# Weights by pairs of column blocks, TensorE in program order, and half of the low parts by ScalarE and an accumulating DMA

## The chip, the cores and the metric

One core of one Trainium2 chip. The metric is the device time of the program in microseconds; the time before is 2558.9 us, the median of three runs (2558.71 to 2560.08).

## The reference

One layer of a decoder trunk on 256 tokens of width 2048 (batch 1), in float32:

```python
h = x + 0.5 * swiglu(rmsnorm(x, ffn1_norm), ffn1_w_gu, ffn1_w_down)      # width 5632
proj = rmsnorm(h, mix_norm) @ w_in                                     # u | v | z | x B C | dt
a_out = chunked_sgu(gelu(u), gelu(v), gm_v_norm, gm_w_s, gm_b_s)        # causal, chunks of 128
m_out = mamba2_group(z, xbc, dt, ...)                                  # conv, scan of 32 heads, gate, norm
h = h + concat([a_out, m_out]) @ w_out
h = h + memory_cross_attention(rmsnorm(h), rmsnorm(mem), w_q, w_kv, w_o)  # 4 heads, 256 memory tokens
h = h + 0.5 * swiglu(rmsnorm(h, ffn2_norm), ffn2_w_gu, ffn2_w_down)
return rmsnorm(h, final_norm)
```

Nearly all the work is `activations @ weights` with 256 rows of activations; some 460 MB of weights are read once from HBM.

## The kernel before, in words

**Arithmetic.** A matrix product in float32 is made of three products in the faster type float32r. Each operand is split exactly into a high part (rounded to float32r) and a low part (the rest): x·w = xh·wh + xh·wl + xl·wh. Weights are split on the fly in `split` (L110): ScalarE copies the raw tile to the high part `whi` (L119), VectorE subtracts it from the raw tile and gives the low part `wlo` (L120). Activations are split when they are transposed to an operand (`to_operand`, L186).

**Tiles.** `load` (L100) brings four k-tiles of 128 rows by 512 columns, 1 MB, into one of three `raw` buffers with one DMA on SyncE's queue. `split` makes two `whi` and two `wlo` tiles of it, each [128, 2, 512]: two k-tiles of one column block. There are four buffers of `whi` and four of `wlo`, so two megabytes are split at a time.

**Projections.** `proj_tok` (L131) computes one block of 512 columns for both token tiles (128 tokens each): for each group of four k-tiles, for each k-tile and token tile, the matmuls of L147 (xh, wh), L148 (xh, wl) and L149 (xl, wh) into the token tile's PSUM bank; the stationary operand is a 128x128 tile of x, the weights move. `proj_feat` (L153) puts features on partitions: the weights are the stationary operand and the 256 tokens move (L164 to L168).

**Order.** The feed-forward parts (`ffn`, L236) alternate a gate block (SiLU by ScalarE, L246) and an up block (product by VectorE, L250), transpose the product to the operand `hid` (L192), and after six or five such blocks project down onto the four 512-column chunks of the residual stream `h`. The mixers use 16 blocks of `w_in` token-wise or feature-wise, with the scan, the gating weights and small transposes between; then `w_out`, the cross attention, and the second feed-forward part with the final norm (`finish`, L667). The program names tiles and dependences; the framework's scheduler orders each engine's instructions by a model of their times and adds the semaphores. TensorE's order is therefore the scheduler's: transposes and small products may be moved among the projections' matmuls. GpSimd makes constants, the powers for the norms (L182), and issues a few loads (`dec` L433, `wn` L518, `mem` L576, `fw` L669).

Of the kernel before, what the change touches and what calls it, by code (L numbers as in the profile page):

```python
# [16 lines left out]
P = 128  # L17
D = 2048
S = 256
# [14 lines left out]
KG = 4  # L34
LOG1P_TERMS = 9

# columns of the packed per-partition parameters
# [8 lines left out]
def hybrid_layer(ctx: ExitStack, tc: tile.TileContext, x, mem, w_gu1, w_dn1, w_in, w_s, w_out,  # L46
# [12 lines left out]

    def slot(shape, dtype, name):  # L60
        return big.tile(shape, dtype, name=name, tag="slot")
# [38 lines left out]
    def load(w, r0, n0, pieces=1):  # L100
        raw = wraw.tile([P, KG, NC], F32, name="raw")
        src = w[r0:r0 + KG * P, n0:n0 + NC].rearrange("(k p) n -> p k n", p=P)
        st = KG // pieces
        for j in range(0, KG, st):
            nc.sync.dma_start(out=raw[:, j:j + st, :], in_=src[:, j:j + st, :])
        return raw

    last_hi = [None]

    def split(raw, behind=None):  # L110
        # behind: for each half, instructions of ScalarE and VectorE to queue it behind
        parts = []
        for j in range(0, KG, 2):
            hi = wsp.tile([P, 2, NC], F32R, name="whi")
            lo = wsp.tile([P, 2, NC], F32R, name="wlo")
            with ExitStack() as order:
                for ins in behind[j // 2] if behind else ():
                    order.enter_context(tc.issue_after(ins))
                last_hi[0] = nc.scalar.copy(out=hi, in_=raw[:, j:j + 2, :]).ins  # L119
                nc.vector.tensor_tensor(out=lo, in0=raw[:, j:j + 2, :], in1=hi.bitcast(F32), op=ALU.subtract)  # L120
            parts.append((hi, lo))
        return parts
# [3 lines left out]
    def load_split(w, r0, n0):  # L126
        key = (id(w), r0, n0)
        return split(*ready.pop(key)) if key in ready else split(load(w, r0, n0))

    # Operands in xts: tiles [P, KG, 2 * S] with the high parts of S tokens, then the low parts.  # L130
    def proj_tok(w, r0, xts, n0, apart=0):  # L131
        # the last `apart` groups run token tile by token tile
        ps = [mm.tile([P, NC], F32, name="acc") for _ in range(NT)]
        groups = [[g] for g in range(len(xts) - apart)]
        if apart:
            groups.append(list(range(len(xts) - apart, len(xts))))
        for gs in groups:
            parts = {g: load_split(w, r0 + g * KG * P, n0) for g in gs}
            order = [(t, g, k) for g in gs for k in range(KG) for t in range(NT)]
            if len(gs) > 1:  # L140
                order.sort()
            for t, g, k in order:
                hi, lo = parts[g][k // 2]
                first, last = g == 0 and k == 0, g == len(xts) - 1 and k == KG - 1
                xh = xts[g][:, k, t * P:(t + 1) * P]
                xl = xts[g][:, k, S + t * P:S + (t + 1) * P]
                nc.tensor.matmul(ps[t], lhsT=xh, rhs=hi[:, k % 2, :], start=first, stop=False)  # L147
                nc.tensor.matmul(ps[t], lhsT=xh, rhs=lo[:, k % 2, :], start=False, stop=False)  # L148
                nc.tensor.matmul(ps[t], lhsT=xl, rhs=hi[:, k % 2, :], start=False, stop=last)  # L149
        return ps  # L150

    # Features on partitions: two tiles of [P, 2, S], for four groups of 128 features.
    def proj_feat(w, xts, n0):  # L153
        ps = [mm.tile([P, 2, S], F32, name="acc") for _ in range(2)]
        for g, xt in enumerate(xts):
            parts = load_split(w, g * KG * P, n0)
            for k in range(KG):
                hi, lo = parts[k // 2]
                first, last = g == 0 and k == 0, g == len(xts) - 1 and k == KG - 1
                for c in range(4):  # L160
                    cs = slice(c * P, (c + 1) * P)
                    o = ps[c // 2][:, c % 2, :]
                    # one accumulation group for both halves of a bank
                    nc.tensor.matmul(o, lhsT=hi[:, k % 2, cs], rhs=xt[:, k, :S], start=first and c % 2 == 0,  # L164
                                     stop=False)
                    nc.tensor.matmul(o, lhsT=hi[:, k % 2, cs], rhs=xt[:, k, S:], start=False, stop=False)  # L166
                    nc.tensor.matmul(o, lhsT=lo[:, k % 2, cs], rhs=xt[:, k, :S], start=False,  # L167
                                     stop=last and c % 2 == 1)  # L168
        return ps

# [14 lines left out]
    # 512 columns of NT token tiles -> one split operand tile, scaled per feature  # L185
    def to_operand(srcs, dst, c0=None):  # L186
        done = []
        for q in range(0, KG, 2):
            ps = side("tpose").rearrange("p (k s) -> p k s", k=2)
            for k in range(2):  # L190
                for t in range(NT):
                    nc.tensor.transpose(out=ps[:, k, t * P:(t + 1) * P],  # L192
                                        in_=srcs[t][:, (q + k) * P:(q + k + 1) * P], identity=ident)
            if c0 is None:
                hi = nc.scalar.copy(out=dst[:, q:q + 2, :S], in_=ps)
                lo = nc.vector.tensor_tensor(out=dst[:, q:q + 2, S:], in0=ps,
                                             in1=dst[:, q:q + 2, :S].bitcast(F32), op=ALU.subtract)
            else:
                for k in range(2):
                    sc = col[:, c0 + q + k:c0 + q + k + 1]  # L200
                    hi = nc.scalar.activation(dst[:, q + k, :S], ps[:, k, :], AF.Copy, scale=sc)
                    lo = nc.vector.scalar_tensor_tensor(out=dst[:, q + k, S:], in0=ps[:, k, :], scalar=sc,
                                                        in1=dst[:, q + k, :S].bitcast(F32),
                                                        op0=ALU.mult, op1=ALU.subtract)
            done.append((hi.ins, lo.ins))
        return done

    class Normed:
        """The next norm's operand, made chunk by chunk as the residual stream gets ready."""
# [5 lines left out]
        def chunk(self, n):  # L215
            self.operand(n)
            self.stats(n)

        def operand(self, n):
            dst = slot([P, KG, 2 * S], F32R, f"xt_{self.name}{n}")  # L220
            self.xts.append(dst)
            return to_operand([h[n][:, t, :] for t in range(NT)], dst, self.c0 + n * KG)
# [7 lines left out]
    def residual(n, ps, scale):  # L230
        for t in range(NT):
            nc.vector.scalar_tensor_tensor(out=h[n][:, t, :], in0=ps[t], scalar=scale, in1=h[n][:, t, :],
                                           op0=ALU.mult, op1=ALU.add)

# [1 line left out]
    def ffn(nrm, w_gu, w_dn, done, before=None, closing=False):  # L236
        for c_from, c_to in ((0, 6), (6, 11)):
            hts = []
            for c in range(c_from, c_to):
                pg = proj_tok(w_gu, 0, nrm.xts, c * NC)  # L240
                if c == 0 and before is not None:
                    before()
                gs = []
                for t in range(NT):
                    g = half_k(F32, "gate")
                    nc.scalar.activation(g, pg[t], AF.Silu, scale=nrm.rstd[:, t:t + 1])  # L246
                    gs.append(g)
                pu = proj_tok(w_gu, 0, nrm.xts, DFF + c * NC)
                for t in range(NT):
                    nc.vector.scalar_tensor_tensor(out=gs[t], in0=pu[t], scalar=nrm.rstd[:, t:t + 1],  # L250
                                                   in1=gs[t], op0=ALU.mult, op1=ALU.mult)
                dst = slot([P, KG, 2 * S], F32R, "hid")
                to_operand(gs, dst)
                hts.append(dst)
            for n in range(4):
                pd = proj_tok(w_dn, c_from * NC, hts, n * NC, apart=2 if closing and c_to == 11 and n == 3 else 0)
                residual(n, pd, 0.5)
                if c_to == 11:
                    done(n)

    n1 = Normed("ffn1", C_FFN1)
    for n in range(4):
        for t in range(NT):
            nc.sync.dma_start(out=h[n][:, t, :], in_=x_v[:, t, n * NC:(n + 1) * NC])
        if n < 3:
# [452 lines left out]
```

## Time and profile before

| | |
|---|---|
| median of three runs | 2558.9 us |
| span of the profiled execution | 2557.8 us |
| TensorE busy, matmuls | 2539.3 us (99%), 12990 |
| VectorE busy | 1375.6 us (54%) |
| ScalarE busy | 1164.2 us (46%) |
| GpSimd busy | 19.8 us (1%) |
| read from HBM | 472.57 MB, 186 GB/s over the span |
| mean granted TensorE clock | 0.999 |

The profiled execution's own time is its span, from the first to the last instruction; what a run takes beyond it (1.1 us against the median) lies outside the instructions. A group's row in the profile gives line, engine, operation, tiles (out<-in), shape and count, then busy time and mean duration in ns, then the idle time of the engine just before, with what ended it. Matmuls are pipelined, so their recorded durations overlap, and the step from one start to the next says what one costs. "PEld" is the load of the stationary operand, "SPq" and "POOLq" are the queues of SyncE and GpSimd.

### The profile page before, as it was taken

To read this page: it belongs to the slowest core of one execution; us is meant where nothing else is said; L and a number is where in the kernel's file an instruction comes from. 1 tells how busy PE (TensorE), PEld (TensorE's weight loads), DVE (VectorE), ACT (ScalarE), POOL (GpSimd) and SP (SyncE) were. 2 spreads that over 40 slices of the span, in tenths; PEclk is the share of its full clock that TensorE was granted. 3 is DMA by queue.
4 is the path that set the end of the run, shared out by engine and by line. 5 is a ranking of instruction groups with operands and counts; after the bars stand their busy time and mean duration, and the time that the engine had idled before them with its cause. 6 is when DMAs were issued, how large, how long until landed. Compare 5 with 4: busy or idle time off the path is not lost.

```text
span 2557.8 us, 31301 instructions
## 1 busy us (share of the span) xinstructions
PE 2539.3 (99%) x12990; PEld 2160.8 (84%) x12990; DVE 1375.6 (54%) x1444; ACT 1164.2 (46%) x1391; POOL 19.8 (1%) x44
## 2 busy tenths in 40 slices
PE   8999999999999999999999999999999999999998
PEld 7888888888889998878888999888888888888887
DVE  5445444545557677755555555555554544445454
ACT  5444434444445455445444544444444443344443
POOL 0000000000000000000000000000000000000000
PEclk9999999999999999999999999999999999999999
DMA  6555555555555555545555655455555555555564
GB/s 236 193 183 193 185 197 196 182 191 188 184 175 173 185 189 190 196 158 190 194 185 182 214 180 167 148 181 177 185 187 192 191 187 194 191 191 189 198 192 145
DMA packets 238704, 476.73 MB, mean 186 GB/s; under 512 B 9713, under 2 KB 9873, under 8 KB 237793
## 3 DMA queue, kind: packets, MB, share of 16 engines
q1 hardware_dynamic: 236736, 465.86, 54.2%
q0 software_dynamic: 1680, 8.73, 1.1%
q8 instruction: 101, 1.65, 0.3%
q14 instruction: 43, 0.34, 0.0%
q10 hardware_dynamic: 144, 0.13, 0.0%
HBM read 472.57 MB, written 2.13 MB: 186 GB/s over the span
## 4 chain that ended last, share of the span: by engine, by line
PE 99%; DMA 0%; issue 0%; SPq 0%; ACT 0%; DVE 0%; ACTq 0%; POOLq 0%; POOL 0%
PE acc L147 27%; PE acc L148 27%; PE acc L149 27%; PE acc L164 5%; PE acc L166 5%; PE acc L167 5%; PE tpose L192 2%; PE yp L456 1%; DMA h<-in_x 0%; PE mixed L521 0%; PE o L654 0%; PE o L652 0%; PE scores L443 0%; PE logits L610 0%; PE logits L611 0%
## 5 line engine op out<-in xcount | busy, mean ns | idle before, releaser
L120 DVE TENSOR_TENSOR wlo<-raw,whi 128x1024 fp32r<-128x1024 f32 x880 | 1076.9, 1225 | 1100.6 <-ACT whi L119 1100.3
L119 ACT CAST whi<-raw 128x1024 fp32r<-128x1024 f32 x880 | 927.4, 1054 | 1253.3 <-PE acc L149 1095.8
L148 PE MATMUL acc<-wlo,xt_ffn 128*128 128x512 f32 x1408 | 550.2, 391 | 0.0
L149 PE MATMUL acc<-whi,xt_ffn 128*128 128x512 f32 x1408 | 550.1, 391 | 0.0
L147 PE MATMUL acc<-whi,xt_ffn 128*128 128x512 f32 x1408 | 548.8, 390 | 0.0
L148 PEld LDWEIGHTS acc<-wlo,xt_ffn 128*128 128x128 f32 x1408 | 264.6, 188 | 54.3
L147 PEld LDWEIGHTS acc<-whi,xt_ffn 128*128 128x128 f32 x1408 | 264.6, 188 | 54.3
L149 PEld LDWEIGHTS acc<-whi,xt_ffn 128*128 128x128 f32 x1408 | 264.7, 188 | 53.6
L148 PE MATMUL acc<-wlo,hid 128*128 128x512 f32 x704 | 274.6, 390 | 0.0
L149 PE MATMUL acc<-whi,hid 128*128 128x512 f32 x704 | 274.5, 390 | 0.0
L147 PE MATMUL acc<-whi,hid 128*128 128x512 f32 x704 | 274.0, 389 | 0.0
L148 PEld LDWEIGHTS acc<-wlo,hid 128*128 128x128 f32 x704 | 132.1, 188 | 27.4
L147 PEld LDWEIGHTS acc<-whi,hid 128*128 128x128 f32 x704 | 132.2, 188 | 27.3
L149 PEld LDWEIGHTS acc<-whi,hid 128*128 128x128 f32 x704 | 132.2, 188 | 26.8
L147 PE MATMUL acc<-whi,xt_mix 128*128 128x512 f32 x384 | 151.7, 395 | 0.0
L149 PE MATMUL acc<-whi,xt_mix 128*128 128x512 f32 x384 | 150.9, 393 | 0.0
L148 PE MATMUL acc<-wlo,xt_mix 128*128 128x512 f32 x384 | 150.0, 391 | 0.0
L164 PE MATMUL acc<-xt_mix,whi 128*128 128x256 f32 x512 | 145.5, 284 | 0.0
L166 PE MATMUL acc<-xt_mix,whi 128*128 128x256 f32 x512 | 145.2, 284 | 0.0
L167 PE MATMUL acc<-xt_mix,wlo 128*128 128x256 f32 x512 | 144.8, 283 | 0.0
L164 PEld LDWEIGHTS acc<-xt_mix,whi 128*128 128x128 f32 x512 | 98.2, 192 | 0.6 <-issue 0.4
L166 PEld LDWEIGHTS acc<-xt_mix,whi 128*128 128x128 f32 x512 | 98.2, 192 | 0.2
(237 smaller groups left out, 2827.7 us busy)
## 6 DMA issues: line engine op xcount, KB each, us to landing
raw<-in_w_gu SPq DMA_DIRECT2D x173, 1024.0 KB, 4.8
raw<-in_w_dn SPq DMA_DIRECT2D x88, 1024.0 KB, 5.1
raw<-in_w_in SPq DMA_DIRECT2D x80, 1024.0 KB, 5.1
raw<-in_w_out SPq DMA_DIRECT2D x32, 1024.0 KB, 5.2
raw<-in_w_kv SPq DMA_DIRECT2D x32, 1024.0 KB, 5.4
raw<-in_w_q SPq DMA_DIRECT2D x16, 1024.0 KB, 5.3
raw<-in_w_o SPq DMA_DIRECT2D x16, 1024.0 KB, 5.1
dec<-cum_rows POOLq DMA_DIRECT2D x4, 1024.0 KB, 5.7
```

Of the source, the lines that this page charges most:

```text
L119: last_hi[0] = nc.scalar.copy(out=hi, in_=raw[:, j:j + 2, :]).ins
L120: nc.vector.tensor_tensor(out=lo, in0=raw[:, j:j + 2, :], in1=hi.bitcast(F32), op=ALU.subtract)
L147: nc.tensor.matmul(ps[t], lhsT=xh, rhs=hi[:, k % 2, :], start=first, stop=False)
L148: nc.tensor.matmul(ps[t], lhsT=xh, rhs=lo[:, k % 2, :], start=False, stop=False)
L149: nc.tensor.matmul(ps[t], lhsT=xl, rhs=hi[:, k % 2, :], start=False, stop=last)
L164: nc.tensor.matmul(o, lhsT=hi[:, k % 2, cs], rhs=xt[:, k, :S], start=first and c % 2 == 0, stop=False)
L166: nc.tensor.matmul(o, lhsT=hi[:, k % 2, cs], rhs=xt[:, k, S:], start=False, stop=False)
L167: nc.tensor.matmul(o, lhsT=lo[:, k % 2, cs], rhs=xt[:, k, :S], start=False, stop=last and c % 2 == 1)
L192: nc.tensor.transpose(out=ps[:, k, t * P:(t + 1) * P], in_=srcs[t][:, (q + k) * P:(q + k + 1) * P], identity=ident)
L456: nc.tensor.matmul(yp[:, i, :], lhsT=dec[:, hh, :], rhs=xdt[:, j * 16 + hh, :], start=True, stop=True)
```

## The change

Three things are changed together.

1. **Pairs of column blocks.** A raw tile holds two k-tiles of two column blocks (gate and up of the same columns, or two neighbouring blocks) instead of four k-tiles of one; it is still 1 MB. `whi` and `wlo` tiles keep their size and hold one k-tile of both blocks. `proj_tok` works on four PSUM tiles (two token tiles by two blocks) and issues six matmuls for each k-tile and token tile: xh with the high and low part of block a, xh with those of block b, then xl with the high part of a and of b. The first and the last group of a projection run token tile by token tile, and each token tile is evacuated (`evac`) when it is complete. The number of matmuls is the same.
2. **TensorE in program order.** Each matmul and transpose is pinned behind the one before it in the program. Side work (transposes of operands, the scan, the gating, the attention's products) is put off by hand: `later(fn, by)` runs `fn` after `by` more groups of a projection.
3. **Low parts by ScalarE and DMA.** Where `src` is given (all groups of `proj_tok` but the first three of the kernel), the low part of the second k-tile is not subtracted by VectorE: ScalarE writes the negative raw weight, rounded to float32r, which is the negative high part, and two DMAs on GpSimd's queue add the float32 weights from HBM onto it, one for each column block (256 KB each). These weights are read from HBM a second time. `proj_feat` keeps VectorE's subtraction for all k-tiles.

The diff, cut to its core:

```diff
+    def pe(ins):
+        return tc.keep_in_program_order(ins)
+    def later(fn, by=1):
+        put_off.append((steps[0] + by, len(put_off), fn))
...
-    def split(raw, behind=None):
-        # behind: for each half, instructions of ScalarE and VectorE to queue it behind
+    def split(raw, behind=(), src=None):
+
         parts = []
-        for j in range(0, KG, 2):
+        for k in range(KP):
             hi = wsp.tile([P, 2, NC], F32R, name="whi")
             lo = wsp.tile([P, 2, NC], F32R, name="wlo")
...
-                last_hi[0] = nc.scalar.copy(out=hi, in_=raw[:, j:j + 2, :]).ins
-                nc.vector.tensor_tensor(out=lo, in0=raw[:, j:j + 2, :], in1=hi.bitcast(F32), op=ALU.subtract)
+                nc.scalar.copy(out=hi, in_=raw[:, k])
+                if src is not None and k == 1:
+
+                    nc.scalar.mul(lo, raw[:, k], -1.0)
+                    for j in range(2):
+                        nc.gpsimd.dma_start(out=lo[:, j], in_=src[j], accum_op=ALU.add)
+                else:
+                    nc.vector.tensor_tensor(out=lo, in0=raw[:, k], in1=hi.bitcast(F32), op=ALU.subtract)
...
+    def proj_tok(w, r0, xts, cs, evac, kts=D // P, apart=1):
...
+            parts = {i: load_split(w, r0 + i * KP * P, cs) for i in pieces}
+            order = [(t, i, k) for i in pieces for k in range(KP) for t in range(NT)]
+            if ng in (0, len(groups) - 1):
                 order.sort()
...
+                matmul(a, xh, hi[:, 0, :], start=first, stop=False)
+                matmul(a, xh, lo[:, 0, :])
+                matmul(b, xh, hi[:, 1, :], start=first)
+                matmul(b, xh, lo[:, 1, :])
+                matmul(a, xl, hi[:, 0, :], start=False, stop=last)
+                matmul(b, xl, hi[:, 1, :], stop=last)
+                if last:
+                    evac(t, ps[t])
+            step()
...
-    ffn(n2, w_gu2, w_dn2, finish, closing=True)
+    ffn(n2, w_gu2, w_dn2, finish, {"apart": 2})
+    step("end")
```

More of the change, by code (lines that the diff above doesn't have):

```diff
@@ L58, in hybrid_layer, with matmul, transpose, step @@
     dram = ctx.enter_context(tc.tile_pool(name="dram", bufs=1, space=DRAM))
+    steps, put_off = [0], []
+    def pe(ins):
+        return tc.keep_in_program_order(ins)
+    def matmul(out, lhsT, rhs, start=False, stop=False):
+        return pe(nc.tensor.matmul(out, lhsT=lhsT, rhs=rhs, start=start, stop=stop))
+    def transpose(out, in_, identity):
+        return pe(nc.tensor.transpose(out=out, in_=in_, identity=identity))
+    def later(fn, by=1):
+        put_off.append((steps[0] + by, len(put_off), fn))
+    def step(to=None):
+        steps[0] += 1
+        for job in sorted(put_off, key=lambda j: j[:2]):
+            if job[0] <= steps[0] or to == "end":
+                put_off.remove(job)
+                job[2]()
     def slot(shape, dtype, name):
@@ L124, in hybrid_layer @@
     ready = {}
[L126 to L140, printed above, removed]
-                order.sort()
[L142 to L150, printed above, removed]
@@ L153, in proj_feat @@
     def proj_feat(w, xts, n0):
         ps = [mm.tile([P, 2, S], F32, name="acc") for _ in range(2)]
[L155 to L159, printed above, removed]
+        for i in range(D // P // (2 * KP)):
+            raw = wraw.tile([P, 2 * KP, NC], F32, name="raw")
+            nc.sync.dma_start(out=raw, in_=w[2 * i * KP * P:2 * (i + 1) * KP * P, n0:n0 + NC].rearrange(
+                "(k p) n -> p k n", p=P))
+            parts = split(raw.rearrange("p (k j) n -> p k j n", j=2))
+            for k in range(2 * KP):
+                kt = 2 * i * KP + k
+                hi, lo = (x[:, k % 2, :] for x in parts[k // 2])
+                xt = xts[kt // KG][:, kt % KG, :]
+                first, last = kt == 0, kt == D // P - 1
@@ L162, in proj_feat @@
                     o = ps[c // 2][:, c % 2, :]
[L164 to L168, printed above, removed]
+                    matmul(o, hi[:, cs], xt[:, :S], start=first and c % 2 == 0, stop=False)
+                    matmul(o, hi[:, cs], xt[:, S:])
+                    matmul(o, lo[:, cs], xt[:, :S], start=False, stop=last and c % 2 == 1)
+            step()
         return ps
@@ L183, in rstd_of @@
         return r
[L186 to L189, printed above, removed]
-            for k in range(2):
[L191 to L206, printed above, removed]
@@ L208, in hybrid_layer, with operand_later, half, first @@
+    def operand_later(srcs, to, name, c0=None, by=1):
+        def half(q):
+            if q == 0:
+                to.append(slot([P, KG, 2 * S], F32R, name))
+            return to_operand(srcs, to[at], q, c0)
+        at = len(to) + sum(1 for o in owed if o is to)
+        owed.append(to)
+        def first():
+            owed.remove(to)
+            assert len(to) == at
+            half(0)
+            later(lambda: half(2), by=0)
+        later(first, by)
+    owed = []
     class Normed:
@@ L228, in stats, with add_proj, evac, ffn @@
                 self.rstd = rstd_of(self.ss, self.name)
[L230 to L236, printed above, removed]
+    def add_proj(w, r0, xts, scale, done=None, **kw):
+        for n in range(0, 4, 2):
+            def evac(t, ps):
+                for j in range(2):
+                    hh = h[n + j][:, t, :]
+                    nc.vector.scalar_tensor_tensor(out=hh, in0=ps[j], scalar=scale, in1=hh, op0=ALU.mult, op1=ALU.add)
+            proj_tok(w, r0, xts, (n * NC, (n + 1) * NC), evac, **(kw if n == 2 else {k: v for k, v in kw.items() if k != "apart"}))
+            if done is not None:
+                done(n)
+                done(n + 1)
+    def ffn(nrm, w_gu, w_dn, done, kw):
         for c_from, c_to in ((0, 6), (6, 11)):
@@ new lines, in hybrid_layer, with evac @@
+    mixed_weights()
+    for g in range(4):
+        later(lambda g=g: make_mixed(g), by=2 + g)
+    ats = []
+    for c in (0, 2):
+        gss = [[], []]
+        def evac(t, ps):
+            for j in range(2):
+                g = half_k(F32, "gate")
+                nc.scalar.activation(g, ps[j], AF.Gelu_apprx_tanh, scale=rstd[:, t:t + 1])
+                nc.vector.scalar_tensor_tensor(out=g, in0=v[t][:, c + j, :],
+                                               scalar=col[:, C_GB + c + j:C_GB + c + j + 1],
+                                               in1=g, op0=ALU.add, op1=ALU.mult)
+                gss[j].append(g)
+        proj_tok(w_in, 0, nx.xts, (U0 + c * NC, U0 + (c + 1) * NC), evac)
+        for j in range(2):
+            operand_later(gss[j], ats, "at", by=1 + j)
@@ L550, in hybrid_layer, with m_operand @@
     rstd_m = rstd_of(ss_m, "m")
     mts = []
[L552 to L553 removed]
+    def m_operand(c):
         gs = []
```

413 lines of the change are left out of this document (218 added, 195 removed).

## The prediction

> **What bounds the kernel now.** I read the page of the profile first (busy time, slices, DMA queues, chain that ended last, costliest groups), then the timeline of one stretch, then the waits and the DMA view.
>
> ```profile
> span 2557.8 us, 31301 instructions
> ...
> PE 2539.3 (99%) x12990; PEld 2160.8 (84%) x12990; DVE 1375.6 (54%) x1444; ACT 1164.2 (46%) x1391; POOL 19.8 (1%) x44
> ...
> q1 hardware_dynamic: 236736, 465.86, 54.2%
> ...
> PE 99%; DMA 0%; issue 0%; SPq 0%; ACT 0%; DVE 0%; ACTq 0%; POOLq 0%; POOL 0%
> ...
> L120 DVE TENSOR_TENSOR wlo<-raw,whi 128x1024 fp32r<-128x1024 f32 x880 | 1076.9, 1225 | 1100.6 <-ACT whi L119 1100.3
> L119 ACT CAST whi<-raw 128x1024 fp32r<-128x1024 f32 x880 | 927.4, 1054 | 1253.3 <-PE acc L149 1095.8
> L148 PE MATMUL acc<-wlo,xt_ffn 128*128 128x512 f32 x1408 | 550.2, 391 | 0.0
> ```
>
> TensorE is the bound: 99% of the chain, no idle time ahead of its large groups. The timeline shows its beat, and ScalarE beside it:
>
> ```profile
> 999.81 0.39 PE L149 MATMUL acc<-whi,xt_mix 128*128 128x512 f32 x1
> 1000.04 0.39 PE L147 MATMUL acc<-whi,xt_mix 128*128 128x512 f32 x1
> 1000.27 0.39 PE L148 MATMUL acc<-wlo,xt_mix 128*128 128x512 f32 x1
> 1000.49 0.39 PE L149 MATMUL acc<-whi,xt_mix 128*128 128x512 f32 x1
> ...
> 1011.83 0.39 PE L148 MATMUL acc<-wlo,xt_mix 128*128 128x512 f32 x1
> ```
>
> ```profile
> 1000.92 1.06 ACT L119 CAST whi<-raw 128x1024 fp32r<-128x1024 f32 x1 [1.66 <-PE acc L149]
> 1003.64 1.06 ACT L119 CAST whi<-raw 128x1024 fp32r<-128x1024 f32 x1 [1.66 <-PE acc L149]
> ```
>
> From 999.81 to 1011.83 lie 53 starts: 226.8 ns from matmul to matmul, whatever the recorded 390 ns (they overlap). Twelve matmuls, the work of one pair of k-tiles here, take 2.72 us, which is also ScalarE's beat (1000.92 to 1003.64). ScalarE waits 1.66 us of it for TensorE to free one of the four high-part buffers: the weights are prepared exactly one ring of buffers ahead. So the change can be judged by two questions: does TensorE issue less, and does the ring still refill in time?
>
> **TensorE's own work.** The number of matmuls, transposes and their shapes is the same in both kernels; the change alters their order. A weight load stands beside every matmul (x12990 each). In the rows above L147 and L148 follow each other with the same stationary operand (the high part of x), and the step between them is 0.23 us, as between L148 and L149, where the operand changes. A longer run of one stationary operand (four instead of two) is therefore worth nothing: 0 us. Changing the PSUM tile from matmul to matmul is worth nothing either: L149 to L147 changes it and takes 0.23 us.
>
> **Side work placed by hand, TensorE in program order.** Transposes and small products now stand one or more groups behind what feeds them.
>
> ```profile
> PEld tpose L192 <- DVE gate L250: 11.1, 44, 0.3
> SPq L105 <- DVE wlo L120: 2122.6, 401, 13.2
> ```
>
> The waits view puts 11.1 us on transposes that wait for the gate product, 44 times. Putting them a group later (5.44 us) removes these waits, but they lie partly under the matmul still running; I take −5 us, with 0 and −11 as ends.
>
> **Start and end.**
>
> ```profile
> 10.72 1.49 PE L192 MATMUL tpose<-ident,h 128*128 128x128 f32 x4 [3.76 <-DMA h<-in_x]
> 11.86 1.20 PE L147 MATMUL acc<-whi,xt_ffn 128*128 128x512 f32 x2
> ...
> 14.14 1.05 PE L192 MATMUL tpose<-ident,h 128*128 128x128 f32 x4
> ```
>
> Today transposes of later chunks of x stand ahead of and among the first matmuls (10.72 to 11.86, and 14.14 for about 1 us). The change puts the later chunks behind whole groups, under cover of loads that have landed by then: −2 us, with 0 and −3.8 (the wait in the first row) as ends. At the end the last projection holds two column blocks, so one more residual update and one more sum of squares stand behind the last matmul:
>
> ```profile
> 2548.54 0.69 DVE L232 SCALAR_TENSOR_TENSOR h<-acc,h 128x512 f32<-128x512 f32 x1 [1.77 <-PE acc L149]
> 2549.26 0.63 ACT L174 ACTIVATE junk<-h 128x512 f32<-128x512 f32 x1 [2.30 <-DVE h L232]
> 2549.80 0.19 ACT L174 ACTIVATION_READ_ACCUMULATOR junk<-h 128x1 f32 x1
> ```
>
> 0.69 on VectorE and 0.63 + 0.19 on ScalarE overlap for the most part: +0.9 us.
>
> **The low parts by ScalarE and DMA.** A token projection reads 1 MB per group of 24 matmuls (5.44 us); there are 376 groups in 44 pairs of column blocks (22 gate/up of 8, 8 down of 12 or 10, 14 others of 8), and all but the first three take the new way for their second k-tile. Per group this removes one subtraction from VectorE (373 × 1.225 = 457 us, off the path, worth nothing) and adds one more ScalarE pass over the same shape (373 × 1.054 = 393 us: ScalarE 1164 to 1557 us, 61%; its 1.66 us of waiting per 2.72 covers it) and two accumulating DMAs of 256 KB, issued on the GpSimd queue. Nothing in the trace accumulates by DMA. The nearest rows are plain 256 KB loads from that queue:
>
> ```profile
> wn<-in_gm_vn POOLq DMA_DIRECT2D x4, 256.0 KB, 3.8
> fw<-in_fin POOLq DMA_DIRECT2D x4, 256.0 KB, 5.6
> ...
> wsr<-in_w_s POOLq DMA_DIRECT2D x1, 256.0 KB, 4.9
> ```
>
> ```profile
> L669 POOL DMA_DIRECT2D fw<-in_fin x4 | 2.2, 550 | 672.3 <-DVE wlo L120 529.7 <-ACT junk L174 98.7 <-PE tpose L192 43.8
> ```
>
> Now the ring. The buffer that the second k-tile's low part uses is freed four k-tiles before. In the middle of a block the time until TensorE needs it is three k-tiles, 36 matmuls × 0.2268 = 8.16 us. In the first and last group of a pair, which run token tile by token tile, it is needed six matmuls earlier: 30 × 0.2268 = 6.80 us. What has to fit is: high part 1.06, negative high part 1.06, the second DMA's issue behind the first 0.55 (the row on GpSimd), and its landing. For the landing the three rows give 3.8 to 5.6. What else the DMA engines carry tells them apart:
>
> ```profile
> 1077.04 14.00 SPq L105 DMA_DIRECT2D raw<-in_w_in  x2
> ```
>
> ```profile
> 1082.13 1.14 POOL L518 DMA_DIRECT2D wn<-in_gm_vn  x2 [1.92 <-DVE y L483]
> ```
>
> ```profile
> 2469.28 5.86 SPq L105 DMA_DIRECT2D raw<-in_w_dn  x2
> ```
>
> ```profile
> 2468.91 0.54 POOL L669 DMA_DIRECT2D fw<-in_fin  x1 [72.06 <-ACT junk L174]
> ```
>
> No weight load was issued between 1077 and about 1090, where the wn loads ran; this fw load and a weight load were issued within 0.4 us of each other. The last reader of the raw tile is now ScalarE's negative pass, so the same event releases the next megabyte on SyncE's queue (today's releaser of that queue is VectorE's low part, the SP row above) and the two accumulating DMAs: they will meet every time. I take fw's 5.6. Upper end: the add must also read its destination, one more pass of 0.524 MB; by the first queue 54.2% of 2557.8 us moved 465.86 MB, 2.98 us per MB, so at most +1.56: 7.2. Lower end: wn's 3.8, and no gain below it.
>
> Chain by 5.6: 2.12 + 0.55 + 5.6 = 8.27 us. Middle groups: 0.11 late per two groups, 285 × 0.05 = 14 us. Edges: 8.27 − 6.80 = 1.47 late, once for each pair of blocks (the wait at one edge gives the next edge its time): 44 × 1.47 = 65 us. By 3.8: 6.47, never late, 0 us. By 4.9: 7.57, edges 0.77, 34 us. By 6.0: 8.67, middle 285 × 0.255 = 73, edges 44 × 1.87 = 82, 155 us. By 7.2: 9.87, every group (9.87 − 8.16) / 2 = 0.86 late, 320 us.
>
> **Sum.** 2557.8 − 5 − 2 + 0.9 + 14 + 65 = 2630.7 us; the profiled span lies 1.1 us under the median of the runs (2558.9), so about 2632: rounded, I say **2630**. With landings between 4.9 (34 us) and 6.0 (155 us) this case alone runs from 2587 to 2708.
>
> **Rivals.**
> - *Hidden (faster).* If the second accumulating DMA lands within 4.1 us of its issue (6.80 − 2.12 − 0.55), the edges are never late, and only the small savings stay: 2558.9 − 5 − 2 + 0.9 = 2553, or 2547 with all 11 us of transpose waits. For it: the wn row (3.8); DMA engines busy 54%. Against it: the fw and wsr rows, and the common releaser. 0.32.
> - *The DMA engines become the bound.* A group moves 1.049 MB of raw weights, 3.12 us of all 16 engines by the 2.98 above, and 0.524 MB more, 1.56 if an accumulating byte costs as much as a plain one: 4.68 of 5.44. If it costs over 1.49 times as much (2.32 / 1.56), the engines set the beat; at twice (a source and a destination read for each byte written), 6.24, 0.80 × 373 = 298 us, 2857. The Trainium skill speaks for it: "Collectives: The Full Stack", the section on the bandwidth ceiling, says that a reduce is half as fast as a copy because the add reads two sources, and gives a measured ratio of 1.93; by that page an estimate of 1.56 × 1.93 = 3.01, 6.13 us per group and 2558.9 + 257 = 2816. No run here shows an accumulating DMA yet. 0.15.
> - *In-order queues block.* GpSimd's few other instructions (x44 in the first fence) or a side product placed too early on TensorE hold an accumulating DMA or the matmuls behind them; some 20 such places (its issues and powers in the mixers, the attention and the last norm) at one or two issues of 0.55 us each: +11 to +22 on the hidden case, 2564 to 2575, with the ring itself in time. 0.08.
> - *Repeated stationary operands are cheaper after all.* A 256-column matmul takes a step of 0.120 us (the rows below), one of 512 columns 0.227: 0.107 for 256 columns leaves 13 ns fixed in each. If a repeated operand saved that, four repeats in six matmuls instead of two would give 9024 / 3 × 13 ns = 39 us, 2520. The equal steps after L147 and L148 speak against it. 0.03.
>
> ```profile
> 1440.01 0.28 PE L166 MATMUL acc<-xt_xa,whi 128*128 128x256 f32 x1
> 1440.13 0.28 PE L167 MATMUL acc<-xt_xa,wlo 128*128 128x256 f32 x1
> ```
>
> **How the numbers follow.** Forecast (ring late) 0.42; hidden 0.32; DMA bound 0.15; in-order 0.08; cheaper operands 0.03. A measurement of this kernel tells about 0.2%, 5 us, from no change (the runs shown span 1.4 us). The hidden case lies on both sides of that line (2547 to 2554, little of it at no change or above): faster 0.21, same 0.11. With the 0.03, faster 0.24; slower 0.65. Range: from the hidden case with all its savings, 2546, to the DMA engines bound just short of twice the plain cost, 2850; the forecast's landings up to 7 us lie in it; the full doubling and the cheaper operands are left out.
>
> **What would show it.** Right: TensorE's idle time before the matmuls of the low part, released by the accumulating DMAs, some 60 to 90 us, most of it in the first or last group of a pair; their time to landing near 5.6 to 6.5 us; 746 DMAs of 256 KB on the GpSimd queue; VectorE near 920, ScalarE near 1560 us busy; the 227 ns step unchanged where nothing waits. DMA bound: weight loads take over 10 us to land, share of the engines above 90%. Hidden: the landings stay under 4.7 us and TensorE remains at 99%. The forecast is wrong if the step itself changes, or if the wait sits on high parts (ScalarE late) or on side work instead.

## The result

The changed kernel takes 2927.6 us (median of four runs, 2924.3 to 2931.9) against 2559.2 us (four runs, 2558.7 to 2560.1): a ratio of 1.144 with an interval of 1.1423 to 1.1455, 368 us slower. The forecast was 2630, its range ended at 2850.

The page of the changed kernel, in the parts that answer to those of before (busy time, slices, queues, chain, groups, DMA issues):

```profile
span 2926.4 us, 33646 instructions
...
PE 2663.9 (91%) x12990; PEld 2177.4 (74%) x12990; DVE 937.1 (32%) x1074; ACT 1504.2 (51%) x1760; POOL 670.9 (23%) x790
...
DMA  8999999998885568789899855798999999999987
...
q1 hardware_dynamic: 188400, 465.87, 45.7%
q0 software_dynamic: 109104, 204.34, 41.2%
...
DMA 44%; PE 43%; ACT 6%; POOL 3%; issue 3%; DVE 1%; ACTq 0%; SPq 0%; POOLq 0%; DVEq 0%
...
L151 ACT ACTIVATE wlo<-raw 128x1024 fp32r<-128x1024 f32 x373 | 396.0, 1062 | 540.9 <-PE acc L69 539.9
L69 PE MATMUL acc<-wlo,xt_ffn 128*128 128x512 f32 x1408 | 566.4, 402 | 73.6 <-DMA wlo<-in_w_gu 71.8
L153 POOL DMA_DIRECT2D wlo<-in_w_gu x346 | 302.0, 1027 | 777.2 <-ACT wlo L151 757.1
...
raw<-in_w_gu SPq DMA_DIRECT2D x346, 512.0 KB, 7.1
raw<-in_w_dn SPq DMA_DIRECT2D x88, 1024.0 KB, 8.2
wlo<-in_w_gu POOLq DMA_DIRECT2D x346, 256.0 KB, 7.1
```

The chain that ended last was TensorE for 99%; now DMA has 44% of it and TensorE 43%, and its largest tiles behind TensorE are the accumulating transfers. The group of low-part matmuls, which waited for nothing, now waits for them. VectorE has lost 438 us of work and ScalarE has gained 340: neither was the bound, and neither has become it. The second queue, which hardly existed, occupies the 16 DMA engines for 41% of the span.

The timeline of a stage of the changed kernel (the output projection of the cross attention) shows one turn of the ring, with only the rows of it that carry it:

```profile
1996.58 1.74 POOL L153 DMA_DIRECT2D wlo<-in_w_o  x2 [3.71 <-ACT wlo L151]
...
1997.25 7.03 SPq L131 DMA_DIRECT2D raw<-in_w_o  x2
...
1998.60 0.39 PE L69 MATMUL acc<-whi,ot 128*128 128x512 f32 x1
...
1999.91 0.50 PE L69 MATMUL acc<-wlo,ot 128*128 128x512 f32 x1 [0.92 <-DMA wlo<-in_w_o]
...
2000.24 0.87 PE L69 MATMUL acc<-whi,ot 128*128 128x512 f32 x3
...
2001.89 1.06 ACT L151 ACTIVATE wlo<-raw 128x1024 fp32r<-128x1024 f32 x1 [2.50 <-PE acc L69]
...
2002.33 0.39 PE L69 MATMUL acc<-wlo,ot 128*128 128x512 f32 x1
...
2002.56 0.39 PE L69 MATMUL acc<-whi,ot 128*128 128x512 f32 x1
...
2002.79 0.39 PE L69 MATMUL acc<-wlo,ot 128*128 128x512 f32 x1
...
2002.85 1.04 ACT L148 CAST whi<-raw 128x1024 fp32r<-128x1024 f32 x1
2003.01 0.84 PE L69 MATMUL acc<-whi,ot 128*128 128x512 f32 x3
...
2003.24 1.74 POOL L153 DMA_DIRECT2D wlo<-in_w_o  x2 [4.93 <-ACT wlo L151]
...
2006.58 0.50 PE L69 MATMUL acc<-wlo,ot 128*128 128x512 f32 x1 [0.92 <-DMA wlo<-in_w_o]
```

Two waiting matmuls stand 6.67 us apart: this group takes 6.67 us instead of 5.44. The step into each is 1.31 us (1998.60 to 1999.91) instead of 0.227. The turn of one buffer takes two groups, here 13.2 us: the wait ends at 1999.91; TensorE frees the buffer and ScalarE starts the negative pass at 2001.89; it ends at 2002.95; GpSimd issues the first transfer at 2003.24 and the second 0.54 later; by the trace's record of landings the second lands 9.26 us after its issue, at 2013.04, and the matmul that waits for it starts at 2013.09. The first of the two lands after 6.90. (This is a long turn; the medians stand below.) The transfers issued at 1996.58 and 1997.12 landed at 2003.47 and 2006.54, the raw load of 1997.25 at 2006.32: the second transfer and the weight load end together. The Trainium skill ("DMA: Bandwidth & Descriptors", "Queues, rings and completion order") says that an engine goes round its queues packet by packet; this common end agrees with it.

Over the whole trace, steps longer than their usual length within the groups of `proj_tok` add up to 353 us: 0.64 us for each of the 244 groups in the middle, 0.84 for the first, 1.13 for the second and 2.52 for the last group of each of the 44 pairs. The largest part, 233 us, stands at the matmul that first reads block b's low part of the second k-tile: the second transfer; 35 us stand at block a's, the first transfer. The first transfer lands after 5.0 us (median), the second after 8.1.

How much time the ring gives can be counted. Block b's half of the buffer is last read by the 22nd of a group's 24 matmuls and first needed by the 16th matmul two groups later (by the 10th where the group runs token tile by token tile). That is 42 steps of 0.2268 us (36 at such an edge); ScalarE starts its negative pass 0.47 us after the start of the freeing matmul (median), so 9.05 us are left, 7.69 at an edge. The chain that has to fit, from the start of the negative pass to the landing of the second transfer, takes 10.0 us in the median: 1.0 us too long for a turn of two groups, 2.3 at an edge.

TensorE also loses time behind its waits. The mean granted clock, the share of TensorE's full clock that the profile shows as granted, is 0.979, against 0.999 before. In 26 stretches, 122 us together, it is half; one of them starts behind the last matmul, and each of the other 25 begins during an idle time of TensorE of 1.5 us or more, or at most 2.3 us behind it (there are 52 such idle times). In the first of them (second fence: a row of the windows view, the granted clock third from its end) matmuls follow each other at 0.43 us instead of 0.227:

```profile
390.52 0.53 PE L69 MATMUL acc<-wlo,hid 128*128 128x512 f32 x1 [1.81 <-DMA wlo<-in_w_dn]
...
394.22 0.63 PE L69 MATMUL acc<-wlo,hid 128*128 128x512 f32 x1
394.65 0.63 PE L69 MATMUL acc<-whi,hid 128*128 128x512 f32 x1
395.07 0.63 PE L69 MATMUL acc<-wlo,hid 128*128 128x512 f32 x1
```

```profile
390.86:397.69 6.83, 5.96 (x15) 4.18 (x14) 1.31 (x3) 1.05 (x1) 0.00 (x0) 0.50 0.77 215
```

Of the 353 us, 267 are steps into a matmul that waited, 40 are steps at half the clock, 25 are the step behind a wait at full clock, and the rest is spread over many small ones. The waits view of TensorE shows less, since the idle time between recorded ends leaves out what the overlap of matmuls hides:

```profile
PE acc L69 <- DMA wlo<-in_w_gu: 71.8, 81, 3.2
PE acc L69 <- DMA wlo<-in_w_dn: 63.8, 57, 2.8
PE acc L69 <- DMA wlo<-in_w_in: 42.5, 32, 5.7
```

### The profile page after: what moved, and what is told of

The parts are those of the page before. It is cut to its first block, busy times and chain, and to the rows that moved or that the text cites. A ratio compares the mean times of both kernels' runs of the same rounds, so it can differ in the third digit from the quotient of the medians.

```text
span 2926.4 us, 33646 instructions
## 1 busy us (share of the span) xinstructions
PE 2663.9 (91%) x12990; PEld 2177.4 (74%) x12990; DVE 937.1 (32%) x1074; ACT 1504.2 (51%) x1760; POOL 670.9 (23%) x790
## 4 chain that ended last, share of the span: by engine, by line
DMA 44%; PE 43%; ACT 6%; POOL 3%; issue 3%; DVE 1%; ACTq 0%; SPq 0%; POOLq 0%; DVEq 0%
PE acc L69 40%; DMA wlo<-in_w_gu 19%; DMA wlo<-in_w_dn 11%; DMA wlo<-in_w_in 6%; ACT wlo L151 5%; DMA wlo<-in_w_out 4%; POOL wlo L153 3%; DMA wlo<-in_w_o 2%; DMA wlo<-in_w_kv 2%; PE tpose L72 1%; ACT whi L148 1%; DMA wn<-in_gm_vn 0%; PE logits L69 0%; PE o L69 0%; DMA raw<-in_w_gu 0%
## 5 line engine op out<-in xcount | busy, mean ns | idle before, releaser
L155 DVE TENSOR_TENSOR wlo<-raw,whi 128x1024 fp32r<-128x1024 f32 x507 | 620.4, 1225 | 1480.4 <-ACT whi L148 1480.0
L69 PE MATMUL acc<-whi,xt_ffn 128*128 128x512 f32 x2816 | 888.7, 394 | 9.3 <-ACT whi L148 9.3
L151 ACT ACTIVATE wlo<-raw 128x1024 fp32r<-128x1024 f32 x373 | 396.0, 1062 | 540.9 <-PE acc L69 539.9
L153 POOL DMA_DIRECT2D wlo<-in_w_gu x346 | 302.0, 1027 | 777.2 <-ACT wlo L151 757.1
L69 PE MATMUL acc<-whi,hid 128*128 128x512 f32 x1408 | 446.9, 397 | 0.0
L153 POOL DMA_DIRECT2D wlo<-in_w_dn x176 | 153.6, 1028 | 426.5 <-ACT wlo L151 407.5
L69 PE MATMUL acc<-xt_mix,whi 128*128 128x256 f32 x1024 | 190.1, 288 | 0.0
L69 PEld LDWEIGHTS acc<-whi,xt_mix 128*128 128x128 f32 x768 | 150.8, 196 | 31.8 <-issue 0.7
L153 POOL DMA_DIRECT2D wlo<-in_w_in x96 | 83.3, 1016 | 391.1 <-ACT wlo L151 382.2
L69 PEld LDWEIGHTS acc<-xt_mix,wlo 128*128 128x128 f32 x512 | 100.3, 196 | 0.0
```

What stands on the lines that cost most here:

```text
L69: return pe(nc.tensor.matmul(out, lhsT=lhsT, rhs=rhs, start=start, stop=stop))
L151: nc.scalar.mul(lo, raw[:, k], -1.0)
L153: nc.gpsimd.dma_start(out=lo[:, j], in_=src[j], accum_op=ALU.add)
L155: nc.vector.tensor_tensor(out=lo, in0=raw[:, k], in1=hi.bitcast(F32), op=ALU.subtract)
```

## The experiments

All times are medians; the kernel before ran beside them at 2559.2 to 2559.7 us. Two theories stand against each other: the **ring** (each low part comes too late because its buffer is only free some 9 us before it is needed, less at the edges) and the **DMA engines** (the added bytes keep them busy for longer than a group takes, and so set the beat). "Stalls" are the long steps within `proj_tok`, as above.

**1. The frame alone**: pairs of blocks, program order, no DMA.

```diff
-                if src is not None and k == 1:
+                if False:
```

> All low parts by VectorE's subtraction; pairs of blocks and program order stay. If the accumulating DMAs cost everything (ring late, or DMA engines full): 2545 to 2560 us, TensorE 99% busy. Rival, the frame or the program order itself costs (side work holds the matmuls): over 2600, with TensorE waiting on transposes or evacuations.

2578.8 us, 1.0075 (1.0060 to 1.0090), outside both ranges that were put down. TensorE is at 99%, stalls 12.6 us. So the frame costs 19.5 us against the 2559.2 of the result (19.0 against the runs beside it), and the low parts by DMA the other 349. TensorE's longest waits in the frame:

```profile
PE acc L69 <- ACT whi L148: 8.5, 1, 8.5
PE tpose L72 <- ACT xf L387: 7.0, 4, 1.9
PE tpose L72 <- DMA h<-in_x: 4.5, 2, 4.2
PE mixed L69 <- DVE v L613: 3.9, 1, 3.9
```

The 11.1 us of transposes that waited for the gate product are gone, as foretold, but transposes of the convolution's output (`xf`) and the gating's products (`mixed`) now wait, with all matmuls behind them.

**2. A deeper ring**: three buffers instead of two for the second k-tile's low part (the room comes from one of three `xin` buffers).

```diff
-            lo = wsp.tile([P, 2, NC], F32R, name="wlo")
+            lo = wsp.tile([P, 2, NC], F32R, name="wlo", tag="wlo_k%d" % k, bufs=2 + k)
...
-    xin = [const.tile([P, PAD + S], F32, name=f"xin{i}") for i in range(3)]
+    xin = [const.tile([P, PAD + S], F32, name=f"xin{i}") for i in range(2)]
```

> The low parts of the second k-tile get a ring of three buffers of their own (five k-tiles, 13.6 us, to refill instead of three, 8.16); the first k-tile's keep two; two instead of three buffers for the convolution's input make the room. Ring theory (a chain of 1.06 + 0.87 + 7.4 us against 8.16 and 6.80): the waits go, 2555 to 2600 us. Engine theory (an accumulating packet of 2 KB takes 178 ns against 84 for a plain one, a group needs 5.5 to 6.2 us of all 16 engines against 5.44): the waits stay or move to the raw tiles, 2700 to 2900 us, DMA share 97% or more.

2628.2 us, 1.0269 (1.0254 to 1.0285), between the two ranges and far nearer to the ring's. One buffer takes away 299.5 of the 349 us, with every byte and every instruction kept; stalls fall from 353 to 57 us. The landings are no shorter (first row); the queues between 100 and 700 us:

```profile
wlo<-in_w_gu POOLq DMA_DIRECT2D x346, 256.0 KB, 7.4
```

```profile
q0 software_dynamic: 30848, 56.15, 53.5%
q1 hardware_dynamic: 48508, 112.63, 52.0%
```

The same view of the changed kernel:

```profile
q0 software_dynamic: 27620, 50.29, 51.2%
q1 hardware_dynamic: 45391, 100.40, 46.7%
```

The windows view of the same stretch (TensorE, its loads, VectorE, ScalarE, GpSimd, granted clock, DMA share, GB/s), the changed kernel first and the deeper ring behind it:

```profile
100.00:700.00 600.00, 556.49 (x2375) 436.12 (x2374) 148.59 (x140) 310.92 (x325) 166.38 (x192) 0.99 0.98 252
```

```profile
100.00:700.00 600.00, 596.06 (x2656) 491.72 (x2654) 164.98 (x155) 344.58 (x361) 185.29 (x214) 1.00 1.06 282
```

In the same 600 us the engines move 12% more with the deeper ring (282 GB/s against 252) and TensorE does 2656 matmuls instead of 2375, although the changed kernel already showed the DMA engines 98% busy. So that share was no sign of the bound.

**3. A plain copy** in place of the add (the low part is then the weight itself).

```diff
-                        nc.gpsimd.dma_start(out=lo[:, j], in_=src[j], accum_op=ALU.add)
+                        nc.gpsimd.dma_start(out=lo[:, j], in_=src[j])
```

> The two GpSimd DMAs copy the weights over the negative high part and do not add (the low part is then the weight itself, so the output is not the layer's). Same bytes from HBM, same issues, same ring. Engine theory: a packet near 84 to 95 ns, 4.1 us per group, landing under 5.5 us, 2555 to 2600 us. Ring theory with the issue and the collision with the raw load as the cause: landing stays near 7 us and the time over 2800 us.

2653.4 us, 1.0366 (1.0351 to 1.0382), between the two ranges: 75 us above the frame, stalls 87. The second transfer lands after 5.5 us instead of 8.1. Same bytes written, same places, same order: the add is worth 274 us by itself in the short ring. The queue of these transfers, from the page:

```profile
q0 software_dynamic: 109104, 204.34, 28.2%
```

**4. The kernel before with the low parts by DMA** for its third and fourth k-tile in the token projections, without the frame.

```diff
+                if src is not None and j == 2:
+                    nc.scalar.mul(lo, raw[:, j:j + 2, :], -1.0)
+                    for i in range(2):
+                        nc.gpsimd.dma_start(out=lo[:, i], in_=src[i], accum_op=ALU.add)
...
```

> The kernel before with one thing changed: the second half of each token projection's low parts by ScalarE's negative high part and two accumulating DMAs of 256 KB (its schedule, single blocks and matmul order stay). If the low parts alone cost the time: 2850 to 2950 us, like the change as a whole. If the pairs of blocks or the program order are needed for the loss (edges run token tile by token tile): 2650 to 2800 us.

2704.9 us, 1.0569 (1.0537 to 1.0600); stalls 148; the second transfer lands after 8.0 us. The same transfers cost 145 us here and 349 in the pair frame, and the chain is as long (10.0 us). The ring gives more time here: the second transfer's data are the fourth k-tile's, which TensorE reads six matmuls (1.36 us) after the third's, and no group runs token tile by token tile. From the freeing matmul to the reading one are 45 steps, less the same 0.47 us: 9.73 us, against 9.05 and 7.69 in the pair frame. This fits the smaller loss; no run tests it by itself.

**5. One transfer of 512 KB** for both blocks.

```diff
-                    for j in range(2):
-                        nc.gpsimd.dma_start(out=lo[:, j], in_=src[j], accum_op=ALU.add)
+                    nc.gpsimd.dma_start(out=lo, in_=src, accum_op=ALU.add)
...
```

> One accumulating DMA of 512 KB for both column blocks instead of two of 256 KB; same bytes, same ring. In the change the second DMA lands 8.6 us after the first one's issue (median), the first after 5.0. If the second issue (0.54 us) is what makes it late: 2840 to 2880 us. If it is the passage through the DMA engines behind the first one and the raw load: 2900 to 2940 us, landing 8 us or more.

2868.2 us, 1.1203 (1.1186 to 1.1220), 59 us less: inside the range for the second issue, though the landing stays near 8 us as in the other case. It lands 7.9 us after its issue in the median (8.2 for the weights of the row below); the second of two landed 8.6 after the issue of the first. So the number of transfers makes less than a tenth of that time, 0.78 us. Block a's half, which landed after 5.0 us, now lands with block b's and is read two matmuls (0.45 us) earlier, and most of the waiting has moved to the matmul that reads it. What is left of the gain is (0.78 − 0.45) / 2 = 0.16 us a group, as measured (59 / 373).

```profile
wlo<-in_w_gu POOLq DMA_DIRECT2D x173, 512.0 KB, 8.2
```

**6. No groups by token tile** (but the last two of the kernel).

```diff
-            if ng in (0, len(groups) - 1):
+            if apart > 1 and ng == len(groups) - 1:
```

> All groups of a projection run k-tile by k-tile (only the closing one keeps token tile by token tile), so the second k-tile is needed after 36 matmuls everywhere, never after 30. If the edges cost what the trace puts on them (2.5 us in each of 44 last groups, 0.84 in each first): 2830 to 2880 us. Rival, the ring as a whole sets the beat and a wait at an edge only takes the place of two others: 2910 to 2940 us.

2844.3 us, 1.1125 (1.1094 to 1.1156), 83 us less. Stalls in the last groups fall from 2.52 to 0.94 us; those in the middle stay at 0.63.

**7. Only block a by DMA**, block b by VectorE.

```diff
-                    nc.scalar.mul(lo, raw[:, k], -1.0)
-                    for j in range(2):
-                        nc.gpsimd.dma_start(out=lo[:, j], in_=src[j], accum_op=ALU.add)
+                    nc.scalar.mul(lo[:, 0], raw[:, k, 0], -1.0)
+                    nc.gpsimd.dma_start(out=lo[:, 0], in_=src[0], accum_op=ALU.add)
+                    nc.vector.tensor_tensor(out=lo[:, 1], in0=raw[:, k, 1], in1=hi[:, 1].bitcast(F32), op=ALU.subtract)
```

> Only column block a of the second k-tile takes the new way (half a negative pass on ScalarE, one accumulating DMA of 256 KB); block b is subtracted by VectorE. Ring theory: 0.6 + 5.0 = 5.6 us, inside 6.80: nothing late, 2580 to 2605 us (the frame alone took 2579). Rival, any accumulating DMA behind a raw load is late: 2650 to 2750 us.

2614.2 us, 1.0211 (1.0196 to 1.0226), between the two ranges: half of the transfers cost 35 us, not half of 349. Its landing fits the window:

```profile
wlo<-in_w_gu POOLq DMA_DIRECT2D x173, 256.0 KB, 4.3
```

**8. Deeper ring and plain copy** together.

> The longer ring of e2 and the plain copy of e3 together (the low part is the weight itself, so the output is not the layer's). e2 took 49 us more than the frame alone. If that rest is the add's load on the DMA engines: 2578 to 2595 us here. If it is the GpSimd queue, ScalarE's pass or the second reading of the weights: 2615 to 2630 us.

2585.7 us (median of three runs; a fourth took 11 ms and is left out), 1.0103 (interval 1.0089 to 1.0129): 6.9 us above the frame, stalls 16. So of the 49 us that the deeper ring left, 42 belong to the add. The queue of these transfers, between 100 and 700 us:

```profile
q0 software_dynamic: 31271, 56.95, 35.2%
```

**9. The frame without program order**: experiment 1 with

```diff
-        return tc.keep_in_program_order(ins)
+        return ins
```

> All low parts by VectorE, as in the run of the frame alone (2578.8 us, ratio 1.0075), but the matmuls and transposes are not pinned in program order: the scheduler orders TensorE as in the kernel before. Theory (the frame's 19.5 us lie at the start, where a square of x on ScalarE stands ahead of the first high parts, and at the end, where two column blocks are evacuated behind the last matmul; the pinned order costs little by itself): 2572 to 2580. Rival (TensorE's fixed order makes it wait for operands that another order would cover): 2558 to 2567.

2562.9 us, 1.0014 (1.0005 to 1.0023). The rival won: 15.8 of the frame's 19.5 us are the program order. TensorE's waits, of this kernel:

```profile
PE tpose L72 <- DMA h<-in_x: 11.4, 3, 6.7
PE mixed L69 <- DVE v L613: 1.7, 1, 1.7
```

The waits for `xf` and for the first high part are gone from it: other matmuls may go ahead. Of the 3.7 us that stay, 3.4 stand at the end: from the start of the last matmul to the end of the span it is 13.1 us, against 9.7 in the kernel before.

**10. The first squares behind the high parts**: experiment 1, with ScalarE's squares of x queued after the last high part that precedes them.

```diff
+    def first_stats(n):
+        with tc.issue_after(last_hi[0]):
+            n1.stats(n)
...
-        later(lambda n=n: n1.stats(n), by=4 + n)
+        later(lambda n=n: first_stats(n), by=4 + n)
```

> All low parts by VectorE; the squares of the chunks of x on ScalarE at the start are queued behind the last high part that precedes them in the program. If the start's part of the frame's cost (the first token matmul at 15.2 us, against 11.9 in the kernel before) comes from ScalarE waiting for the second chunk of x, the first matmul returns to about 12 us and the time is 2574 to 2576. If the loads of the weights themselves arrive later, it stays at 2578 to 2580.

2574.5 us, 1.0054 (1.0037 to 1.0071), 4.3 us less than experiment 1. There, on ScalarE, a square waits for x and the first high parts stand behind it:

```profile
13.14 0.63 ACT L226 ACTIVATE junk<-h 128x512 f32<-128x512 f32 x1 [4.98 <-DMA h<-in_x]
...
14.12 1.98 ACT L148 CAST whi<-raw 128x1024 fp32r<-128x1024 f32 x2
```

and TensorE's first token matmul starts at 15.21; with the squares behind, it starts at 10.09:

```profile
10.09 0.79 PE L69 MATMUL acc<-whi,xt_ffn 128*128 128x512 f32 x1 [3.03 <-ACT whi L150]
```

The earlier start (5.1 us) is clear in the trace. The 4.3 us in the total are not clear of noise, since the intervals of the two experiments overlap.

**11. The frame without groups by token tile**: experiment 1 with the edit of experiment 6.

> All low parts by VectorE; the first and the last group of a projection are no longer run token tile by token tile (but for the last two groups of the kernel). If the edges cost the frame its ring time (30 matmuls instead of 36), the few us of waits in the projections go: about 2574. If the edges are what gives the PSUM banks time to be evacuated, four banks are now freed at once and the next pair's first matmuls wait for ScalarE and VectorE: 44 pairs by 0.3 to 1 us, 2590 to 2620.

2586.9 us, 1.0105 (1.0090 to 1.0120), between the two ranges and 8 us more than experiment 1; the two intervals touch. So the token tiles one after the other seem to help a little where nothing waits for a DMA. But the waits that the second case named are hardly there (1.3 us on a gate's evacuation); the 8 us are spread over small steps, and their cause stays open.

**12. Deeper ring, only block a by DMA.**

> The deeper ring (three buffers for the second k-tile's low part instead of two, and two x buffers instead of three) with one accumulating DMA of 256 KB for block a; block b's low part by VectorE. Theory (two costs: the ring's length, and the load of the adding transfers on the DMA engines): with the ring long enough and half of the adding bytes, the engines need 3.1 + 0.8 x 2.1 = 4.8 us of 5.44 per group, so the time is that of the frame alone, 2579 to 2586. Rival (the accumulating transfer costs time of its own, by ScalarE's or GpSimd's queue or by its own latency, even when there is a buffer to spare): 2600 to 2614, as with one block and the short ring (2614).

2586.9 us, 1.0106 (1.0091 to 1.0121), 1 us above the theory's range: 27 us less than the short ring's 2614, and stalls of 16 us. The transfer costs nearly nothing where a buffer is to spare; 8 us above the frame remain, of which 4.2 stand in one longer wait of `mixed`:

```profile
PE mixed L69 <- DVE v L613: 8.1, 1, 8.1
```

No version here beats the kernel before; the best, the frame without program order, is 3.7 us behind it.

## Why the prediction was wrong

- **The step that failed** is "I take fw's 5.6" for the landing. The way it went, slower because the ring is late, was the forecast's; a term of its sum had the wrong size. The second transfer landed after 8.1 us in the median. fw's row was a good price for a plain transfer beside a weight load: experiment 3 has 5.5 us, and the add is worth 274 us there. Taking a plain transfer for an adding one was the error; the upper end of 7.2, one more pass over the destination, was nearer and still short.
- **The ring was the right cause, but its working had two more sizes wrong.** That the buffer decides is shown by experiment 2: 299.5 of 349 us. ScalarE puts the negative pass ahead of the high part, so the chain holds one pass of 1.06 us less than was counted: 1.06 + 0.29 + 0.54 + 8.1 = 10.0. And the ring gives 9.05 and 7.69 us, not 8.16 and 6.80, since the buffer is free, and needed, inside a k-tile's twelve matmuls and not at their ends. Both errors make the ring look tighter than it is. With the trace's sizes a landing of 5.6 us gives a chain of 7.5, which fits even at the edges, and not 79 us; with the working's sizes a landing of 8.1 would be (10.77 − 8.16) / 2 = 1.3 us late in every group, some 490 us.
- **Two near hits are luck.** The line for 7.2 us gives 320 us, and the stalls beyond the frame's are 353 − 12.6 = 341: a landing too short and a ring too tight cancel, and the 341 hold some 65 us of half clock and of steps behind waits that the working did not have. Experiment 3 cost 75 us where the working for 5.6 gives 14 + 65 = 79: by the trace's sizes its median chain of 7.5 us is nowhere late, so its stalls come from transfers that land later than the median and from steps at half the clock (13 us).
- **Edges.** "Most of it in the first or last group" was wrong at this landing: 156 us lie in the middle groups, 50 in the second ones and 148 in the first and last ones. With a chain of 10 us even the middle groups are late.
- **The rival of the DMA engines** had the price about right and the consequence wrong. Between 100 and 700 us of the deeper ring the adding queue takes 53.5% of 600 us for 56.15 MB, 5.72 us per MB; the kernel before took 2.98 per MB of plain weights: 1.92 times. The Trainium skill gives a ratio of 1.93 for a reduce against a copy ("Collectives: The Full Stack", the section on the bandwidth ceiling). The trace agrees only if the plain weight load is taken for the copy. Against the copy of experiment 8, which differs by the add alone, it is 1.54 times: 35.2% of the same 600 us for 56.95 MB, 3.71 us per MB. At 5.72 us per MB a group needs 3.12 + 0.524 × 5.72 = 6.1 us, as the rival worked out, but TensorE was not held to it: experiment 2 loses 49 us beyond the frame, not 257 or 298. The two queues' times add up to 105.5% of the engines' time there, so packets of the two overlap, and a sum of their times is no bound.
- **Hidden** was wrong by the landing; experiment 12 shows that the transfer hides with half the bytes and a buffer more. **Cheaper repeated operands** is excluded by the timeline: the matmuls at 2002.33, 2002.56 and 2002.79, with one stationary operand, and the next at 2003.01 follow each other at 0.22 to 0.23 us. **In-order queues** had the right mechanism at the wrong places: not GpSimd's issues but transposes and products in TensorE's own order, 15.8 us.
- **Small terms.** Transposes −5: the waits named are gone, but the pinned order brings others, with the start +15.8. Start −2: it came out later (some 4 us to be had by experiment 10). End +0.9: 3.4 by the trace. All three are wrong in size, two in sign; together they are 20 of the 368 us. A lower clock behind long waits was not among the terms; 40 us of the changed kernel's long steps stand in it.

## What to carry to other kernels

An operation that the trace does not show needs a price of its own: a plain transfer of the same size was no stand-in for an adding one here. Then compare the whole chain from the freed buffer to the landing with the time that the ring gives, and count that time from the last matmul that reads the buffer to the first that needs it again; one buffer was worth 300 us here. A number that comes out right can hide two errors that cancel; look where the waits stand. Work moved off an engine that is no bound gains nothing and costs whatever its new place makes late; and a fixed order on the busiest engine turns each late operand of side work into its idle time.

## What the runs showed of the hardware

- An adding packet of 2 KB takes 178 ns in the median on a DMA engine, a plain one of the weight loads 84 (packet records of the changed kernel), one of experiment 3's copies 99.
- GpSimd is busy for 1.03 us with each issue of an adding transfer (its group above) against 0.54 us for a plain one in experiment 3.
- The first matmul after a wait takes longer: from 1999.91 to 2000.24 are 0.33 us, where 0.227 is usual. Of the changed kernel's 353 us of long steps, 25 stand in the step behind one that waited.
- Behind about half of TensorE's idle times of 1.5 us or more (25 of 52 in the changed kernel) the granted clock is half for a stretch, 3.4 us in most of them, and a matmul of 512 columns takes a step of 0.43 us instead of 0.227.
